# Delta-net layer of a decoder step: the norm of a head's output in two groups of chunks, on VectorE but for the power

## The chip, the cores and the metric

The kernel runs on one core of a Trainium2 chip. The metric is the device time of one execution in microseconds; the median of three runs before the change is 3306.21 us (3305.95 to 3306.49).

## The reference

One inference step of a two-layer decoder, for a prompt of 1024 tokens and, beside it, 8 sequences of 8 new tokens each (64 rows). Layer 0 mixes tokens with a gated delta net, layer 1 with windowed attention, and both end in a feed-forward block. Only the delta net's output norm is touched by the change. For each of 8 heads (128 wide) the recurrence is

```
def step(s, xs):
    w_c, u_c, attn_c, q_c, k_c, ge_c = xs
    u = u_c - jnp.einsum('bhcd,bhde->bhce', w_c, s)
    o = jnp.einsum('bhcd,bhde->bhce', q_c, s) + jnp.einsum('bhcs,bhse->bhce', attn_c, u)
    s = ge_c[..., None, None] * s + jnp.einsum('bhcd,bhce->bhde', k_c, u)
    return s, o
...
o = rms_norm(o, o_gain) * jax.nn.silu(gate...)
y = o.reshape(b, l, A_V_DIM).astype(h.dtype) @ w_out
```

`rms_norm` divides each token's row of `o` by the root of its mean square plus 1e-6. In the kernel `q` is not normalised before the recurrence, so its inverse length `rq` (one number per token, with the factor 1/sqrt(128)) enters in the norm: the mean square is multiplied by `rq` twice, and the factor applied to the row is the power -0.5 of that, times `rq` again.

## The kernel before, in words

Tokens lie in nine chunks: eight of 128 rows for the prompt, one of 64 for the new tokens (`NT`, `tok`). The delta net (`gdn`) is a pipeline over heads. In step `i` of its loop three generators run merged: `gdn_scan` of head `i-2` (the recurrence, its decode part, the norm and the output), `gdn_prep` of head `i-1` (squares, the inverse of the chunk matrix, `kdec`, `vs`, `aT`), and `gdn_dense` of head `i` (three projections of 72 matmuls each in three pieces of columns, 384, 352 and 352, with the convolution `yc` on VectorE). The `yield` values decide which generator goes next; after that the compiler's scheduler places every instruction in the queue of its engine by its own estimates, and each engine works through its queue in that order. So an instruction that waits holds back all that stands behind it in its queue. Six steps (heads 0 to 5 of the order) have all three generators; in the last two the dense work has ended and the gate projections stand in its place.

What the prediction speaks of, by name:

- `o` shares its tile with `vs`, so the profile writes `vs` for both. L1210 adds up chunk `c` of the output (`vs<-t,C`), L1201 updates the state `S`, L1188 makes `r`, L1186 is the product of the keys with `S`.
- L1223 squares a chunk on ScalarE and sums it into a column of `ss_o`. L1224 to L1228, all on GpSimd (POOL), turn nine columns into the factor `f_o`; L1227 is the power. L1231 multiplies `o` by `f_o`, also on POOL. L1239 transposes the chunks on TensorE (PE) into `ot` (bank tag `C`), and `ot` goes to DRAM.
- L1068 transposes `E` into `F` on VectorE (DVE), and L1074 `B<-F,NZ` is the first product with it, in the inversion of the next head's chunk matrix. Its results pass through ScalarE and VectorE and come back to PE as `B<-Y,Dx`.
- L1141 multiplies `kqm` on POOL for the decode part of the next scan, from `qT` and `kT`, which SP loads by DMA. L144 makes the low part `w` of the next weights, L978 evicts `kdec` from PSUM, which frees a bank for L1007 `A<-kT`.
- L983 subtracts in `aT`, whose rows come by a broadcast DMA from `gcd`.

The instructions of the norm, in the order of the code:

```
nc.gpsimd.tensor_tensor(ss, ss, rq, op=ALU.mult)
nc.gpsimd.tensor_tensor(ss, ss, rq, op=ALU.mult)
nc.gpsimd.tensor_scalar(ss, ss, 1.0 / P, EPS, op0=ALU.mult, op1=ALU.add)
nc.gpsimd.tensor_tensor(f, ss, half, op=ALU.pow)
nc.gpsimd.tensor_tensor(f, f, rq, op=ALU.mult)
```

Of the kernel before, what the change touches and what calls it, by code (L numbers as in the profile page):

```python
# [16 lines left out]
AF = mybir.ActivationFunctionType  # L17
ALU = mybir.AluOpType
# [4 lines left out]
P = 128  # L23
# [4 lines left out]
SD = DB * DL  # L28
T = SP + SD
NT = 9  # L30
FF = 2816
NF = FF // P
EPS = 1e-6
# [6 lines left out]
def tok(tt):  # L40
    return (tt * P, P) if tt < 8 else (SP, SD)
# [592 lines left out]
class Gdn:  # L634
# [473 lines left out]
    def gdn_scan(self, v, wk, slot, m, st, og, qkv, delta_p, delta_s, on, oT):  # L1108

        nc = self.nc  # L1110
        ident, hd = self.ident, v["hd"]
        kdec, vs, aT, T2, bcol, rq = (v[x] for x in ("kdec", "vs", "aT", "T2", "bcol", "rq"))
        ge, gam, ngam = st["ge"], st["gam"], st["ngam"]
        bc = lambda col, s, rows=P, n=P: col[:rows, s][:, :, None].to_broadcast([rows, s.stop - s.start, n])
        parts = ((slice(0, 8), P), (slice(8, 9), SD))

        def rtile(name, bufs=2):
            return wk.tile([P, P], F32, tag=name, name=name, bufs=bufs)

        def small(name):  # L1120
            return wk.tile([P, NT], F32, tag=name, name=name, bufs=2)

        def quad(name):
            return wk.tile([P, 4, P], F32, tag="quad", name=name, bufs=4)
# [4 lines left out]
        o = vs  # L1129
        S = None  # L1130

        def decode():
            sd, kq = [], []
            for g in range(2):
                s_d, kqm = quad("s_d"), quad("kqm").rearrange("p b (x t) -> p b x t", x=2)
                sd.append(s_d)
                kq.append(kqm)
                nc.sync.dma_start(s_d, v["state"][:, 4 * g:4 * g + 4])
                q8 = m["Q8"][:, 4 * g:4 * g + 4].rearrange("p b c l -> p b (c l)")
                for x, f in ((0, kT), (1, qT)):  # L1140
                    nc.gpsimd.tensor_tensor(kqm[:, :, x], f[:, None, SP:T].to_broadcast([P, 4, SD]), q8, op=ALU.mult)  # L1141
            yield
            p1 = self.bank("C")
            for g in range(2):
                for b in range(4):
                    nc.tensor.matmul(p1[:, :P], kq[g][:, b].rearrange("p x t -> p (x t)"), sd[g][:, b],
                                     start=g + b == 0, stop=g == 1 and b == 3)
            r = rtile("rd", 1)
            nc.vector.scalar_tensor_tensor(r[:SD], p1[:SD, :P], ngam[:SD, 8, hd:hd + 1], vs[:SD, 8], op0=ALU.mult, op1=ALU.add)
            t = rtile("td", 1)  # L1150
            nc.scalar.activation(t[SD:], p1[SD:, :P], AF.Copy, scale=gam[SD:, 8, hd:hd + 1])
            yield
            p2 = self.bank("C")
            nc.tensor.matmul(p2[:SD, :P], T2[:SD, 8, :SD], r[:SD], start=True, stop=True)
            u = rtile("ud", 1)
            nc.scalar.activation(u[:SD], p2[:SD, :P], AF.Copy, scale=bcol[:SD, 8:9])
            yield
            p4 = self.bank("C")
            nc.tensor.matmul(p4[:SD, :P], aT[:SD, 8, :SD], u[:SD], start=True, stop=True)
            nc.vector.tensor_add(o[:SD, 8], p4[:SD, :P], t[SD:])  # L1160
            yield
            ums = []
            for g in range(2):
                b4 = slice(4 * g, 4 * g + 4)
                um = quad("um")[:SD]
                ums.append(um)
                nc.vector.tensor_tensor(um, u[:SD][:, None, :].to_broadcast([SD, 4, P]),
                                        m["sel8"][:, b4, None].to_broadcast([SD, 4, P]), op=ALU.mult)
                nc.gpsimd.tensor_tensor(sd[g], sd[g], ge[:, 1, b4, hd][:, :, None].to_broadcast([P, 4, P]), op=ALU.mult)
            yield  # L1170
            for g in range(2):
                b4 = slice(4 * g, 4 * g + 4)
                p3 = self.bank("C")
                w = p3.rearrange("p (b d) -> p b d", d=P)
                nc.tensor.matmul(w, kdec[:SD, 8], ums[g], start=True, stop=True)
                nc.vector.tensor_add(sd[g], sd[g], w)
                nc.sync.dma_start(delta_s[b4, hd].rearrange("b k v -> k b v"), sd[g])
                yield

        dec = decode()  # L1180
        for c in range(8):
            t0 = c * P
            r = vs[:, c]
            if c:
                p1 = self.bank("C")
                nc.tensor.matmul(p1[:, :P], kT[:, t0:t0 + P], S, start=True, stop=True)  # L1186
                r = rtile("r")
                nc.vector.scalar_tensor_tensor(r, p1[:, :P], ngam[:, c, hd:hd + 1], vs[:, c], op0=ALU.mult, op1=ALU.add)  # L1188
                yield 0.02
                next(dec, None)  # L1190
                yield 0.01
            p2 = self.bank("C")
            nc.tensor.matmul(p2[:, :P], T2[:, c], r, start=True, stop=True)
            u = rtile("u")
            nc.scalar.activation(u, p2[:, :P], AF.Copy, scale=bcol[:, c:c + 1])
            yield 0.03
            p3 = self.bank("C")
            nc.tensor.matmul(p3[:, :P], kdec[:, c], u, start=True, stop=True)
            So, S = S, rtile("S")
            if c:  # L1200
                nc.vector.scalar_tensor_tensor(S, So, ge[:, 0, c, hd:hd + 1], p3[:, :P], op0=ALU.mult, op1=ALU.add)  # L1201
            else:
                nc.vector.tensor_copy(S, p3[:, :P])
            p4 = self.bank("C")
            nc.tensor.matmul(p4[:, :P], aT[:, c], u, start=True, stop=True)
            if c:
                nc.tensor.matmul(p4[:, P:2 * P], qT[:, t0:t0 + P], So, start=True, stop=True)
                t = rtile("t1")
                nc.scalar.activation(t, p4[:, P:2 * P], AF.Copy, scale=gam[:, c, hd:hd + 1])
                nc.vector.tensor_add(o[:, c], t, p4[:, :P])  # L1210
            else:
                nc.vector.tensor_copy(o[:, c], p4[:, :P])
            yield 0.03
        nc.sync.dma_start(delta_p[hd], S)
        for _ in dec:
            pass
        half = self.mhalf[:, :NT]
        ss, f = small("ss_o"), small("f_o")
        nc.gpsimd.memset(ss, 1.0)
        for c in range(NT):  # L1220
            n = tok(c)[1]
            j = rtile("junk")
            nc.scalar.activation(j[:n], o[:n, c], AF.Square, accum_out=ss[:n, c:c + 1])  # L1223
        nc.gpsimd.tensor_tensor(ss, ss, rq, op=ALU.mult)  # L1224
        nc.gpsimd.tensor_tensor(ss, ss, rq, op=ALU.mult)
        nc.gpsimd.tensor_scalar(ss, ss, 1.0 / P, EPS, op0=ALU.mult, op1=ALU.add)
        nc.gpsimd.tensor_tensor(f, ss, half, op=ALU.pow)  # L1227
        nc.gpsimd.tensor_tensor(f, f, rq, op=ALU.mult)  # L1228
        yield 0.1
        for s, n in parts:  # L1230
            nc.gpsimd.tensor_tensor(o[:n, s], o[:n, s], bc(f, s, n), op=ALU.mult)  # L1231
        yield 0.1
        ot = slot("ot", "kT2").rearrange("p a b -> p (a b)")
        for c0, c1 in GR:
            ps = self.bank("C")
            n = 0
# [645 lines left out]
```

## Time and profile before

| what | value |
|---|---|
| median of three runs | 3306.21 us |
| the profiled execution | 3316.33 us |
| its span in the profile | 3314.6 us |
| mean granted clock of TensorE | 0.967 of full speed |
| busy share PE / DVE / ACT / POOL | 94% / 65% / 46% / 41% |

The span runs from the first to the last instruction that the profiler saw; 1.7 us of the execution lie around it. The delta net takes roughly the stretch from 60 to 790 us. Busy shares are means over stages with different limits. A timeline row gives the start in us from the span's start, the duration, the engine, the line, the operation with its output and inputs, the shape, how often it stands there, and in brackets the idle time of the engine before it with what ended it. The granted clock is a share of 2.4 GHz: 1.00 is 2.4 GHz and 0.50 is 1.2 GHz.

### The profile page before, as it was taken

The page shows a single profiled execution, that of the slowest core. Times are in us where ns is not written, and L with a number is a line of the kernel's source. Part 1 is how long each engine was busy: PE and PEld are TensorE (multiplying, and loading weights), DVE is VectorE, ACT ScalarE, POOL GpSimd, SP SyncE. Part 2 cuts the span into 40 slices and gives each one's busy share as a digit, 9 for nine tenths or more (in the row PEclk, how much of TensorE's full clock was granted, in tenths as well). Part 3 has the DMA queues.
Part 4 walks back from the last instruction along what each step waited for, and adds up shares of the span by engine and source line. Part 5 has one row for each costly group of instructions (what it writes and reads, how often), then busy time and mean ns, then how long its engine had stood idle before and what let it go on. Part 6 is the DMA issues. An engine that isn't in the chain of part 4 may idle for free. (4 is left out here: it accounts for less than half of the span.)

```text
span 3314.6 us, 54654 instructions
## 1 busy us (share of the span) xinstructions
PE 3101.6 (94%) x20072; PEld 2841.4 (86%) x20072; DVE 2154.9 (65%) x4483; ACT 1527.0 (46%) x3739; POOL 1354.0 (41%) x1374
## 2 busy tenths in 40 slices
PE   7899999999999999999999999998898999999997
PEld 7888888888789999987788988888586999998785
DVE  5676676633666666566847777677746666665766
ACT  5444455433533333244547676767334333332344
POOL 3233333333456666544531223130114566664543
PEclk9999999999999999999999999999889999999998
DMA  4333333345322222363451111111443122224534
GB/s 136 95 109 101 101 101 101 103 130 172 124 73 90 98 98 91 130 200 86 140 164 47 33 54 53 35 54 52 156 130 118 65 98 98 97 96 151 168 104 131
DMA packets 283752, 346.42 MB, mean 105 GB/s; under 512 B 43330, under 2 KB 218802, under 8 KB 280668
## 3 DMA queue, kind: packets, MB, share of 16 engines
q1 hardware_dynamic: 271612, 293.51, 28.7%
q0 software_dynamic: 11728, 48.87, 3.8%
q8 instruction: 158, 2.59, 0.3%
q14 instruction: 110, 0.90, 0.1%
q10 hardware_dynamic: 144, 0.56, 0.0%
HBM read 245.21 MB, written 97.66 MB: 103 GB/s over the span
## 5 line engine op out<-in xcount | busy, mean ns | idle before, releaser
L784 PE MATMUL mm<-h_hi,w 128*128 128x352 f32 (+1 forms) x1536 | 444.9, 349 | 11.0 <-ACT xr L821 8.6
L451 PE MATMUL acc<-wa,ga 128*128 128x512 f32 x1716 | 418.5, 398 | 23.4 <-ACT wa L389 14.2
L451 PEld LDWEIGHTS acc<-wa,ga 128*128 128x128 f32 x1716 | 326.4, 192 | 102.8 <-ACT wa L389 15.8
L1366 PE MATMUL mm<-h_hi,w 128*128 128x352 f32 (+1 forms) x1152 | 353.8, 342 | 0.0
L784 PEld LDWEIGHTS mm<-h_hi,w 128*128 128x128 f32 x1536 | 283.6, 193 | 23.0 <-ACT xr L821 9.5
L784 PE MATMUL mm<-h_lo,w 128*128 128x352 f32 (+1 forms) x768 | 260.1, 339 | 0.0
L303 DVE TENSOR_TENSOR s<-w,s 128x512 fp32r<-128x512 f32 x132 | 190.9, 1447 | 101.8 <-ACT s L302 101.6
L302 ACT ACTIVATE s<-t 128x512 fp32r<-128x512 f32 x176 | 110.8, 630 | 301.5 <-PE mm L354 287.9
L390 DVE TENSOR_TENSOR ga<-graw,ga 128x512 fp32r<-128x512 f32 (+2 forms) x176 | 153.0, 874 | 131.0 <-ACT ga L389 130.7
L322 POOL TENSOR_TENSOR wide<-wide,v 128x288 f32<-128x288 f32 (+1 forms) x176 | 148.2, 842 | 199.5 <-DVE v L321 199.1
L389 ACT ACTIVATE ga<-graw 128x512 fp32r<-128x512 f32 (+2 forms) x176 | 100.9, 576 | 259.1 <-PE acc L451 234.4
L1457 ACT ACTIVATE s<-s,stat 128x128 f32<-128x128 f32 (+1 forms) x384 | 169.6, 443 | 95.4 <-DVE stat L1455 93.5
L1366 PEld LDWEIGHTS mm<-h_hi,w 128*128 128x128 f32 x1152 | 211.8, 189 | 1.6
L144 POOL TENSOR_TENSOR w<-raw,w 128x1024 fp32r<-128x1024 f32 x38 | 100.5, 2646 | 244.7 <-ACT w L141 162.6
L303 DVE TENSOR_TENSOR s<-t,s 128x512 fp32r<-128x512 f32 x176 | 161.7, 920 | 46.1 <-ACT s L302 45.8
L1366 PE MATMUL mm<-h_lo,w 128*128 128x352 f32 (+1 forms) x576 | 189.1, 328 | 0.0
L587 PE MATMUL mm<-mw_hi,o_hl 128*128 128x512 f32 x544 | 177.3, 403 | 3.9 <-ACT o_hl L575 3.9
L293 POOL TENSOR_TENSOR t<-w 128x512 f32<-128x512 f32 x88 | 115.2, 1311 | 146.5 <-DVE s L303 65.1
L1474 DVE TENSOR_TENSOR pl<-tr,ph 128x256 fp32r<-128x256 f32 (+1 forms) x192 | 104.6, 545 | 105.1 <-ACT ph L1473 104.0
L354 PE MATMUL mm<-b0h,s 128*128 128x256 f32 (+1 forms) x704 | 145.2, 293 | 12.2 <-ACT s L302 9.5
L831 DVE SCALAR_TENSOR_TENSOR yc<-xr,convw,yc 128x1112 f32<-128x1112 f32 x72 | 115.5, 1604 | 54.5 <-ACT yc L829 54.4
L784 PEld LDWEIGHTS mm<-h_lo,w 128*128 128x128 f32 x768 | 149.1, 194 | 1.9 <-issue 0.9
(474 smaller groups left out, 9329.4 us busy)
## 6 DMA issues: line engine op xcount, KB each, us to landing
w<-in_ffn_w_in_dram SPq DMA_DIRECT2D x88, 512.0 KB
graw<-gs SPq DMA_DIRECT2D x143, 256.0 KB
gs<-wide POOLq DMA_DIRECT2D x22, 1024.0 KB, 4.2
gs<-wide POOLq DMA_DIRECT2D x66, 256.0 KB, 2.6
raw<-in_a_w_in_dram SPq DMA_DIRECT2D x32, 512.0 KB
qkv<-f SPq DMA_DIRECT2D x24, 544.0 KB
xo<-x SPq DMA_DIRECT2D x24, 512.0 KB
raw<-in_b_w_q_dram SPq DMA_DIRECT2D x24, 512.0 KB
```

The lines of the kernel that those rows point to most:

```text
L293: op(t, x, y)
L302: nc.scalar.activation(out[j][:, 0], x, AF.Copy)
L303: nc.vector.tensor_sub(out[j][:, 1], x, out[j][:, 0])
L322: nc.gpsimd.tensor_tensor(out, out, v, op=ALU.mult)
L354: nc.tensor.matmul(ps[:, :HC[c][1]], u, v, start=z == 0, stop=z == 11)
L390: nc.vector.tensor_sub(t[:, 1, :n], x, t[:, 0, :n])
L451: nc.tensor.matmul(acc[i], g[:, u, c], w[:, v], start=p == 0 and n == 0, stop=p == NP - 1 and n == 2)
L587: nc.tensor.matmul(ps, a, b[:, k], start=k == 0 and i == 0, stop=k == KD - 1 and i == len(seq) - 1)
L784: nc.tensor.matmul(ps[:, :n], a[:, k, :], b[:, k, n0:n0 + n], start=i_ == 0, stop=i_ == 23)
L831: nc.vector.scalar_tensor_tensor(yc, xr[:, j:j + CW], w(j), yc, op0=ALU.mult, op1=ALU.add)
L1366: nc.tensor.matmul(ps[:, :n], a[:, k, :], b[:, k, n0:n0 + n], start=i == 0, stop=i == 23)
L1457: nc.scalar.activation(s[:, a, :n], s[:, a, :n], AF.Exp, bias=m, scale=-1.0, accum_out=stat[:, 1, a, b:b + 1])
```

## The change

The nine columns of the norm are made in two groups: chunks 0 to 3 while the scan is at chunk 5 (their scaling at chunk 6), and chunks 4 to 8 at the end. The three small multiplications and the multiply-add go to VectorE, and so does the scaling of `o`; the power stays on GpSimd. The memset of `ss_o` moves to the start of the scan.

```diff
--- before.py
+++ after.py
@@ -1112,7 +1112,6 @@
         kdec, vs, aT, T2, bcol, rq = (v[x] for x in ("kdec", "vs", "aT", "T2", "bcol", "rq"))
         ge, gam, ngam = st["ge"], st["gam"], st["ngam"]
         bc = lambda col, s, rows=P, n=P: col[:rows, s][:, :, None].to_broadcast([rows, s.stop - s.start, n])
-        parts = ((slice(0, 8), P), (slice(8, 9), SD))
 
         def rtile(name, bufs=2):
             return wk.tile([P, P], F32, tag=name, name=name, bufs=bufs)
@@ -1177,8 +1176,35 @@
                 nc.sync.dma_start(delta_s[b4, hd].rearrange("b k v -> k b v"), sd[g])
                 yield
 
+        half = self.mhalf[:, :NT]
+        ss, f = small("ss_o"), small("f_o")
+        nc.gpsimd.memset(ss, 1.0)
+
+        def norm(c0, c1):
+
+            s = slice(c0, c1)
+            for c in range(c0, c1):
+                n = tok(c)[1]
+                j = rtile("junk")
+                nc.scalar.activation(j[:n], o[:n, c], AF.Square, accum_out=ss[:n, c:c + 1])
+            for _ in range(2):
+                nc.vector.tensor_tensor(ss[:, s], ss[:, s], rq[:, s], op=ALU.mult)
+            nc.vector.tensor_scalar(ss[:, s], ss[:, s], 1.0 / P, EPS, op0=ALU.mult, op1=ALU.add)
+            nc.gpsimd.tensor_tensor(f[:, s], ss[:, s], half[:, s], op=ALU.pow)
+            nc.vector.tensor_tensor(f[:, s], f[:, s], rq[:, s], op=ALU.mult)
+            yield
+            for x, n in ((slice(c0, min(c1, 8)), P), (slice(max(c0, 8), c1), SD)):
+                if x.start < x.stop:
+                    nc.vector.tensor_tensor(o[:n, x], o[:n, x], bc(f, x, n), op=ALU.mult)
+
         dec = decode()
         for c in range(8):
+            if c == 5:
+                mid = norm(0, 4)
+                next(mid)
+            if c == 6:
+                for _ in mid:
+                    pass
             t0 = c * P
             r = vs[:, c]
             if c:
@@ -1214,21 +1240,11 @@
         nc.sync.dma_start(delta_p[hd], S)
         for _ in dec:
             pass
-        half = self.mhalf[:, :NT]
-        ss, f = small("ss_o"), small("f_o")
-        nc.gpsimd.memset(ss, 1.0)
-        for c in range(NT):
-            n = tok(c)[1]
-            j = rtile("junk")
-            nc.scalar.activation(j[:n], o[:n, c], AF.Square, accum_out=ss[:n, c:c + 1])
-        nc.gpsimd.tensor_tensor(ss, ss, rq, op=ALU.mult)
-        nc.gpsimd.tensor_tensor(ss, ss, rq, op=ALU.mult)
-        nc.gpsimd.tensor_scalar(ss, ss, 1.0 / P, EPS, op0=ALU.mult, op1=ALU.add)
-        nc.gpsimd.tensor_tensor(f, ss, half, op=ALU.pow)
-        nc.gpsimd.tensor_tensor(f, f, rq, op=ALU.mult)
+        end = norm(4, NT)
+        next(end)
         yield 0.1
-        for s, n in parts:
-            nc.gpsimd.tensor_tensor(o[:n, s], o[:n, s], bc(f, s, n), op=ALU.mult)
+        for _ in end:
+            pass
         yield 0.1
         ot = slot("ot", "kT2").rearrange("p a b -> p (a b)")
         for c0, c1 in GR:
```

The scheduler's order moves with it. First POOL at the end of a head. Before (L1224 to L1231 are the norm; `kqm` follows them):

```order
L144 TENSOR_TENSOR w<-raw,w 128x1024
L996 MEMSET nc 64x16
L1224 TENSOR_TENSOR ss_o<-ss_o,rq 128x9
L1225 TENSOR_TENSOR ss_o<-ss_o,rq 128x9
L1226 TENSOR_SCALAR ss_o<-ss_o 128x9
L1227 TENSOR_TENSOR f_o<-ss_o,mhalf 128x9
L1228 TENSOR_TENSOR f_o<-f_o,rq 128x9
L1219 MEMSET ss_o 128x9
L1231 TENSOR_TENSOR vs<-vs,f_o 128x1024
L1231 TENSOR_TENSOR vs<-vs,f_o 64x128
L1141 TENSOR_TENSOR kqm<-qT_2303,Q_501 128x4x64
```

With the change:

```order
L144 TENSOR_TENSOR w<-raw,w 128x1024
L996 MEMSET nc 64x16
L1140 TENSOR_TENSOR kqm<-qT_2309,Q_501 128x4x64
L815 MEMSET xr 128x3
L1193 TENSOR_TENSOR f_o<-ss_o,mhalf 128x5
L1181 MEMSET ss_o 128x9
```

All of the norm but the power has left this queue, and `kqm` and a memset of `xr` now stand ahead of the power of the last five columns.

VectorE at the end of a head, from `Dx` to the group of `aT`. Before:

```order
L1052 TENSOR_TENSOR Dx<-dc,sel_458 128x1024
L831 SCALAR_TENSOR_TENSOR yc<-xr,convw,yc 128x1112
L1052 TENSOR_TENSOR Dx<-dc,sel_458 64x64
L816 COPY xr<-hist 128x8x3
L1079 TENSOR_TENSOR E<-dc,par 128x256
L983 SCALAR_TENSOR_TENSOR aT<-aT,gc,U 128x128
L1068 STREAM_TRANSPOSE F<-E 128x256
L983 SCALAR_TENSOR_TENSOR aT<-aT,gc,U 128x128 x7
```

With the change:

```order
L1052 TENSOR_TENSOR Dx<-dc,sel_458 128x1024
L1052 TENSOR_TENSOR Dx<-dc,sel_458 64x64
L1191 TENSOR_TENSOR ss_o<-ss_o,rq 128x5
L1079 TENSOR_TENSOR E<-dc,par 128x256
L1192 TENSOR_SCALAR ss_o<-ss_o 128x5
L983 SCALAR_TENSOR_TENSOR aT<-aT,gc,U 128x128
L1194 TENSOR_TENSOR f_o<-f_o,rq 128x5
L1068 STREAM_TRANSPOSE F<-E 128x256
L1198 TENSOR_TENSOR vs<-vs,f_o 128x512
L1198 TENSOR_TENSOR vs<-vs,f_o 64x128
L983 SCALAR_TENSOR_TENSOR aT<-aT,gc,U 128x128 x7
```

The three steps ahead of the power are put between older instructions; the multiplication of `f_o`, which needs the power, stands ahead of the transposition into `F`.

VectorE in the scan, where the first group is made. Before:

```order
L1034 TENSOR_TENSOR vs<-A,ivk 128x512
L1040 STREAM_SHUFFLE row<-dc 128x144
L1201 SCALAR_TENSOR_TENSOR S<-S,ge,C 128x128
L1041 TENSOR_TENSOR row<-row,nc 128x9x4
L1042 TENSOR_TENSOR dc<-dc,row 128x9x4
L1040 STREAM_SHUFFLE row<-dc 128x144
```

With the change:

```order
L1034 TENSOR_TENSOR vs<-A,ivk 128x512
L1192 TENSOR_SCALAR ss_o<-ss_o 128x4
L1040 STREAM_SHUFFLE row<-dc 128x144
L1194 TENSOR_TENSOR f_o<-f_o,rq 128x4
L1227 SCALAR_TENSOR_TENSOR S<-S,ge,C 128x128
L1041 TENSOR_TENSOR row<-row,nc 128x9x4
L1198 TENSOR_TENSOR vs<-vs,f_o 128x512
L1042 TENSOR_TENSOR dc<-dc,row 128x9x4
```

The multiplication of `f_o` stands ahead of the state `S`, and the scaling of four chunks behind it. On PE the chunk transposes at the end of a head were one group of six ahead of `B<-F,NZ`:

```order
L784 MATMUL mm<-h_hi,w 128x352
L1239 MATMUL C<-ident,vs 128x128 x6
L1074 MATMUL B<-F,NZ 128x128 x8
L1074 MATMUL B<-Y,Dx 128x128 x4
L784 MATMUL mm<-h_hi,w 128x352
```

With the change:

```order
L784 MATMUL mm<-h_hi,w 128x352
L1255 MATMUL C<-ident,vs 128x128 x2
L784 MATMUL mm<-h_hi,w 128x352
L784 MATMUL mm<-h_lo,w 128x352
L784 MATMUL mm<-h_hi,w 128x352
L1255 MATMUL C<-ident,vs 128x128 x2
L784 MATMUL mm<-h_hi,w 128x352
L784 MATMUL mm<-h_lo,w 128x352
L784 MATMUL mm<-h_hi,w 128x352
L1074 MATMUL B<-F,NZ 128x128 x8
L1074 MATMUL B<-Y,Dx 128x128 x4
L1255 MATMUL C<-ident,vs 128x128 x4
```

Four transposes and six dense matmuls now stand ahead of `B<-F,NZ`, and the other transposes behind it.

## Rows read from the trace of the kernel before

**Rows 1.** Waits of PE from 100 to 780 us: us in all, times, longest.
```profile
PE C L1239 <- POOL vs L1231: 26.0, 7, 4.1
PE A L1007 <- DVE kdec L978: 11.6, 6, 2.0
```

**Rows 2.** Timeline of PE, second of six like heads: start, us, instruction, [idle before].
```profile
289.33 0.48 PE L784 MATMUL mm<-h_hi,w 128*128 128x352 f32 x2
289.65 0.32 PE L784 MATMUL mm<-h_lo,w 128*128 128x352 f32 x1
...
294.25 1.54 PE L1239 MATMUL C<-ident,vs 128*128 128x128 f32 x6 [4.11 <-POOL vs L1231]
295.58 0.64 PE L1074 MATMUL B<-F,NZ 128*128 128x128 f32 x2
```

**Rows 3.** Timeline of POOL in the same stretch.
```profile
289.27 2.65 POOL L1227 TENSOR_TENSOR f_o<-ss_o,mhalf 128x9 f32<-128x9 f32 x1
...
292.30 2.30 POOL L1231 TENSOR_TENSOR vs<-vs,f_o 128x1024 f32<-128x1024 f32 x2
294.57 0.72 POOL L1141 TENSOR_TENSOR kqm<-qT,Q 128x256 f32<-128x256 f32 x1
```

**Rows 4.** Timeline of DVE in the same stretch.
```profile
289.05 1.21 DVE L1052 TENSOR_TENSOR Dx<-dc,sel 128x1024 f32<-128x1024 f32 x1
...
291.74 0.42 DVE L1079 TENSOR_TENSOR E<-dc,par 128x256 f32<-128x256 f32 x1
292.32 2.03 DVE L983 SCALAR_TENSOR_TENSOR aT<-aT,gc,U 128x128 f32<-128x128 f32 x1 [0.16 <-DMA aT<-gcd]
294.27 0.43 DVE L1068 STREAM_TRANSPOSE F<-E 128x256 f32<-128x256 f32 x1
```

**Rows 5.** Timelines of DVE, POOL and PE, fourth like head, after the end.
```profile
476.83 3.31 DVE L831 SCALAR_TENSOR_TENSOR yc<-xr,convw,yc 128x1112 f32<-128x1112 f32 x1
475.47 3.49 POOL L144 TENSOR_TENSOR w<-raw,w 128x1024 fp32r<-128x1024 f32 x1 [2.78 <-ACT w L141]
481.40 0.49 PE L1007 MATMUL A<-kT 128*128 128x128 f32 x2 [2.01 <-DVE kdec L978]
```

**Rows 6.** Stretches: busy us, granted clock (PEclk), DMA share, GB/s.
```profile
242.40:245.70 3.30, 3.29 (x14) 3.30 (x15) 1.87 (x8) 0.75 (x2) 2.84 (x6) 0.50 1.05 346
481.40:484.70 3.30, 3.29 (x27) 3.30 (x28) 2.54 (x9) 1.09 (x3) 2.84 (x6) 1.00 1.05 346
```

**Rows 7.** Timeline of DVE in the scan of the second head.
```profile
268.54 0.20 DVE L1029 TENSOR_SCALAR rq<-rq 128x9 f32<-128x9 f32 x1 [0.38 <-POOL rq L1028]
...
270.30 0.69 DVE L1034 TENSOR_TENSOR vs<-A,ivk 128x512 f32<-128x512 f32 x1 [0.20 <-PE A L954]
...
271.17 0.35 DVE L1201 SCALAR_TENSOR_TENSOR S<-S,ge,C 128x128 f32<-128x128 f32 x1
```

**Rows 8.** Timeline of PE there.
```profile
271.74 0.38 PE L1186 MATMUL C<-S,kT 128*128 128x128 f32 x2
```

**Rows 9.** Power of 1 column and of 9 on POOL, by line: duration min/median/max.
```profile
L153 POOL TENSOR_TENSOR rstd<-rstd,mhalf x72: 541/549/1602, 7.1 to 3307.3; 128x1 f32<-128x1 f32 x64, 64x1 f32<-64x1 f32 x8
L1028 POOL TENSOR_TENSOR rq<-nq,mhalf x8: 1794/1796/2975, 115.8 to 666.3; 128x9 f32<-128x9 f32 x8
```

**Rows 10.** DMA packets, second head, 290.3 to 293.5 and 293.5 to 293.6 us.
```profile
DMA packets 956, 0.96 MB, mean 299 GB/s; under 512 B 48, under 2 KB 828, under 8 KB 956
DMA packets 59, 0.03 MB, mean 302 GB/s; under 512 B 0, under 2 KB 59, under 8 KB 59
```

**Rows 11.** DMA packets, fifth like head, 528.8 to 532.7 us.
```profile
DMA packets 950, 0.98 MB, mean 251 GB/s; under 512 B 48, under 2 KB 815, under 8 KB 950
```

**Rows 12.** Timeline of POOL, fifth like head.
```profile
533.62 0.78 POOL L1141 TENSOR_TENSOR kqm<-qT,Q 128x256 f32<-128x256 f32 x1 [0.93 <-DMA qT<-qkv]
534.34 0.10 POOL L815 MEMSET xr<- 128x3 f32 x1
```

**Rows 13.** Timeline of PE, last head.
```profile
761.74 0.66 PE L1239 MATMUL C<-ident,vs 128*128 128x128 f32 x4 [1.33 <-POOL vs L1231]
```

## The prediction

> **What bounds the kernel now.** The profile's first part (the table above) has PE busy for 94% of the span, so the question is what PE waits for where the change is made. The view of PE's waits over the delta net names two. It waited 26.0 us in seven places for POOL's scaling of `o` (tile `vs`, L1231) and 11.6 us in six for `kdec` [rows 1]. The timelines show the first: at the end of the second head PE issues its last dense product at about 290.1 and then stands still for 4.11 us, because the transposes of L1239 are next in its queue [rows 2]. POOL meanwhile works through the power of nine columns, 2.65 us, and the scaling, 2.30 us [rows 3]. Six heads are alike in this. Two more facts from the same stretch count. VectorE's `aT` at 292.32 takes 2.03 us beside POOL's scaling, so `F` comes only at 294.27, and PE's `B<-F,NZ` could start at 295.58 without waiting [rows 2, 4]. And `kqm` follows the scaling on POOL at once [rows 3].
>
> The second wait comes later in the step. VectorE's `yc` takes 3.31 us beside POOL's `w` of 3.49 us, `kdec` stands behind it, and PE waits 2.01 us [rows 5]. Of two such places the stretch behind one ran at a granted clock of 0.50 (1.2 GHz) for 3.3 us, the one shown from the fourth head at 1.00 (2.4 GHz) [rows 6].
>
> **Part one, the first group, during the scan.** Removed: nothing here. Added: four short operations on VectorE, the power of four columns on POOL and the scaling of 512 elements a row on VectorE. The order has `f_o<-f_o,rq` ahead of the state `S`, and it needs the power. So the chain is: the last `vs<-A` ends at 270.30 + 0.69 = 270.99; the multiply-add takes 0.20, as `rq` did [rows 7]; the power takes, by 549 ns for one column and 1796 ns for nine, 0.549 + 3 x 0.156 = 1.02 us [rows 9]; the multiplication 0.20; then `S`, 0.35 [rows 7]. `S` would end at 270.99 + 0.20 + 1.02 + 0.20 + 0.35 = 272.76. The product with the keys, which started at 271.74 without idle time [rows 8], would start at about 272.8: 1.05 us later, and everything on PE behind it too, since PE's order has the same two dense products ahead of it as before. Queued behind the waiting multiplication are `S`, the `row` and `dc` steps of the next head and the scaling. The scaling itself costs 0.69, as `vs<-A` of the same shape [rows 7]; it stands behind `S` and I cost it at nothing, since six dense products and a decode product lie between `C<-S,kT` and the next product that needs VectorE. Without that cover it is 0.7 more. The least is 0 (if the scheduler's dense work hides all), the most about 1.75. I take 1.05, the chain's own sum: **six heads, +6.3 us**.
>
> **Part two, the end of a head.** Removed from POOL: three small multiplications, a multiply-add, four columns of the power and the scaling. VectorE gets the small ones and the scaling of five chunks, behind `F`, and PE takes the transposes of finished chunks first, then six dense products, then `B<-F,NZ`. If this were all, the stall would be gone. But POOL's queue now has `kqm` and a memset ahead of the power, and `kqm` needs `qT` from DMA, while VectorE's `f_o` stands ahead of `F`, which PE's next product needs. So a load decides. In the second head it moved as packets between 2 and 8 KB: 956 less 828 is 128 of them from 290.3 to 293.5, and none in the tenth behind (59 of 59 are smaller) [rows 10]. In the fifth head the packets of this size end by 532.7 as well (950 less 815: the 128 and 7 of the next transfer) [rows 11], and there `kqm` did wait for `qT`, and started at 533.62 [rows 12], 0.9 us behind the last packet. With the same 0.9, `qT` is there at 294.4 in the second head: just before `kqm` started, at 294.57, and not earlier.
>
> The chain is then: `kqm` at 294.45, 0.72 long [rows 3]; the memset, 0.10 [rows 12]; the power of five columns, 0.549 + 4 x 0.156 = 1.17 [rows 9]; the multiplication, 0.20 [rows 7]; `F`, 0.43 [rows 4]. That gives 297.07, so `B<-F,NZ` starts at about 297.1 and not at 295.58: +1.5. PE has six dense products less to do behind it, at 0.48 - 0.32 = 0.16 each [rows 2], so 0.94 are won; two transposes more are left for later, at 1.54 / 6 = 0.26 by row or some 0.22 with the overlap of their ends, so 0.44 are lost [rows 2]. Net 1.5 - 0.94 + 0.44 = 1.0. The least is 0.05: `kqm` at 293.5, at once on the last packet. The most is 2.0: in the fifth head the load came 0.9 behind the scaling's end instead of level with it [rows 12]. I take 1.0, since the second head's load is the one whose packets and start both stand in the rows: **six heads, +6.0 us**. The stall of PE does not go, it changes its name: some 5.5 us for `F` from VectorE.
>
> On VectorE the end costs 0.69 for 512 elements and about 0.28 for the new tokens; both stand behind `F` and beside PE's own products of the inversion, so nothing. At 65% busy VectorE has the room.
>
> **Part three, `kdec`.** `kqm` from `kT` and `w` change places on POOL, and the dense products that were pulled forward are missing as filler there. The wait of 2.0 us [rows 1] may go from nothing lost to all gone: -12 to +6 us over six heads. The nearest row is the wait as it is, so I keep it, but in heads where the clock fell behind it a shift decides, and a stretch of 3.3 us at half clock [rows 6] is 1.65 us dearer. I take **-2.0 us** in all, about one such stretch.
>
> **Part four, the last head.** There is no next head to prepare, and PE waits 1.33 us for the scaling [rows 13]. On VectorE with half the chunks done that goes: **-1.3 us**.
>
> **The sum.** 6.3 + 6.0 - 2.0 - 1.3 = +9.0 us. The sum is made against the profiled execution, 3316.33 us (span 3314.6 and 1.7 around), which gives 3325.3. That execution stands 10.1 above the median of the runs, 3306.21, so on the median it is **3315.2 us**.
>
> **A rule against the rows.** Both a rule and this sum speak of the same scaling. By the rows it took 2.30 us on POOL [rows 3], and VectorE multiplied as many elements a row (1024) in 1.21 [rows 4]. The Trainium skill, "GPSIMD Engine Reference", § 4.1 Engine selection, puts elementwise work with two inputs on VectorE and calls it about twice slower on GpSimd; these two rows agree. By the exchange alone the sum would be, per head, 2.30 - 1.21 = 1.1 and 2.65 - 1.17 = 1.5 for the shorter power, 2.6 less, and 15.6 + 1.3 = 16.9 less in all: 3289.3. I go by the queue instead, because an instruction's price matters only if it starts on time.
>
> **The rivals.** *The end is shorter after all* (0.2). If `qT` lands before POOL wants it, the power starts on its inputs: `E` ends at 291.74 + 0.42 = 292.16 [rows 4], the multiply-add at 292.36, power 293.53, multiplication 293.73, `F` 294.16, `B<-F` about 294.2: -1.4 - 0.94 + 0.44 = -1.9 a head. Then 6.3 - 11.4 - 2.0 - 1.3 = -8.4, or 3297.8. It decides from the point where `qT` is there by about 291.5, 2.9 us earlier than now. For it: nothing forbids the other loads to shift. Against it: the packets [rows 10, 11]. The exchange by itself (3289.3) is its far end.
>
> *The mid group costs little and the `kdec` wait halves* (0.25). If PE's dense work takes up all but 0.3 us of the late `S`, and a shorter queue on POOL takes `w` from beside `yc` in half the heads, it is 1.8 + 6.0 - 6.0 - 1.3 = +0.5, or 3306.7: no change. For it: `yc` beside `w` is a matter of 2 us [rows 5]. Against it: PE had no idle time ahead of `C<-S,kT` [rows 8], so its order is tight there.
>
> *The clock falls more often* (0.1). The stall at the end grows and one is added in the scan. If each new one is followed by a stretch at half clock, as behind `kdec` [rows 6], six times 1.65 come on top: 3325.1. Against it: the stretch from the fourth head stayed at 1.00 behind a longer wait than the new one in the scan.
>
> **How the numbers follow.** The forecast has 0.45. A measurement of this kernel tells about 0.2% from no change, 6.6 us. Faster by more: the first rival, 0.2. Within: the second, 0.25, and the forecast's lower part where the end costs its least, 0.05, so 0.3. Slower by more: the rest of the forecast and the third, 0.5. The forecast's own range is 3306 to 3321; with the rivals and the end at its most, 3294 to 3326.
>
> **What would show it.** Right: in the changed kernel PE waits for VectorE's `F` at `B<-F,NZ` in six places, over 5 us each, in place of POOL's `vs`; POOL's `kqm` has idle time for `qT` ahead of it and the power starts behind; PE waits about 1 us at one `C<-S,kT` in each of six heads. Wrong: no wait at `B<-F,NZ`, or a power that runs before `kqm` could; no wait in the scan; a wait for `kdec` that is gone, or a new one elsewhere in the queue of VectorE.

## The result, and the profile after

The changed kernel took 3324.69 us in the median of five runs (3319.43 to 3333.98), against 3306.26 for the kernel before: a ratio of 1.0053 (95% interval 1.0035 to 1.0071). Measured once more later, beside the experiments, it took 3320.31 us against 3307.31, a ratio of 1.0032 (1.0019 to 1.0045). So it is slower by 0.2 to 0.7%, some 13 to 18 us; the forecast was 9 us slower. The first median lies above the forecast's own range of 3306 to 3321 us and inside the wide one of 3294 to 3326; the second lies in both. The runs of the kernel before itself spread from 3297 to 3321 us in the later sessions, so only ratios over many runs are compared below.

The profiled execution of the changed kernel has a span of 3318.1 us, only 3.5 more than that of before, which was itself 10 us above its median. The stretch from `B<-F,NZ` of the first like head to that of the last head tells more. It holds nearly the same work in both, and here stands with its length, the busy times of PE, PE's weight loads, VectorE, ScalarE and POOL (with counts of instructions), the granted clock, DMA share and GB/s, first before the change:

```profile
216.40:693.70 477.30, 437.10 (x2932) 401.81 (x2932) 326.57 (x912) 237.46 (x736) 165.68 (x204) 0.96 0.33 103
```

and after it:

```profile
213.30:701.10 487.80, 440.64 (x2926) 403.25 (x2927) 325.29 (x978) 236.60 (x735) 139.47 (x177) 0.95 0.32 101
```

It is 10.5 us longer (7.0 in the second profile of the changed kernel). PE stands idle 7.0 us more (47.2 for 40.2; 4.1 in the second profile) and is busy 3.5 us longer with nearly the same instructions, at a lower clock (2.9 in the second). POOL is busy 26 us less, and that bought nothing. What PE waited for in the delta net, in us, with times and longest, after the change:

```profile
PE B L1074 <- DVE F L1068: 21.7, 6, 3.9
PE mm L784 <- ACT xr L821: 13.4, 8, 2.9
PE C L1212 <- DVE S L1229: 6.0, 3, 2.0
PE C L1212 <- DVE S L1227: 5.2, 8, 0.8
...
PE A L1007 <- DVE kdec L978: 3.6, 3, 1.8
```

The 26.0 us for POOL's scaling [rows 1] are gone by name. In their place stand 21.7 for `F`, six new waits for `xr` (the list had two waits of 4.8 us for `xr` before), and 5.2 for the state `S`. The 11.6 for `kdec` [rows 1] have become 3.6, but 6.0 for the first `S` of a head are new. (In the second profile it is 20.5 for `F`, 5.4 for `S`, 6.2 for `kdec` and 2.4 for the first `S`.)

The second head shows how. PE's timeline, which answers to [rows 2]:

```profile
288.83 0.38 PE L1255 MATMUL C<-ident,vs 128*128 128x128 f32 x2
290.74 0.43 PE L784 MATMUL mm<-h_hi,w 128*128 128x352 f32 x1 [1.53 <-ACT xr L821]
...
295.92 3.75 PE L1074 MATMUL B<-F,NZ 128*128 128x128 f32 x16 [3.73 <-DVE F L1068]
```

VectorE in the same stretch [rows 4]:

```profile
291.03 0.16 DVE L1192 TENSOR_SCALAR ss_o<-ss_o 128x5 f32<-128x5 f32 x1
291.60 0.35 DVE L983 SCALAR_TENSOR_TENSOR aT<-aT,gc,U 128x128 f32<-128x128 f32 x1 [0.41 <-DMA aT<-gcd]
295.26 0.17 DVE L1194 TENSOR_TENSOR f_o<-f_o,rq 128x5 f32<-128x5 f32 x1 [3.31 <-POOL f_o L1193]
295.34 0.44 DVE L1068 STREAM_TRANSPOSE F<-E 128x256 f32<-128x256 f32 x1
295.70 0.84 DVE L1198 TENSOR_TENSOR vs<-vs,f_o 128x512 f32<-128x512 f32 x2
```

and POOL [rows 3]:

```profile
293.33 0.72 POOL L1140 TENSOR_TENSOR kqm<-qT,Q 128x256 f32<-128x256 f32 x1 [5.32 <-DMA qT<-qkv]
293.99 0.11 POOL L815 MEMSET xr<- 128x3 f32 x1
294.05 1.17 POOL L1193 TENSOR_TENSOR f_o<-ss_o,mhalf 128x5 f32<-128x5 f32 x1
```

Read from below: POOL stands idle for 5.32 us, because `kqm` waits for `qT`. The input of the power is ready at 291.19 and the power starts at 294.05. VectorE waits 3.31 us for it with `F` behind, although `E` was done at 291.1. (This head lies some 1.2 us earlier than in the profile before: POOL's `w` ahead of it ends at 284.31 here and at 285.47 there. So `kqm`'s 293.33 answers to the 294.45 of the forecast.) PE waits 3.73 us for `F`. Ahead of that PE waits 1.53 us for `xr`, a wait that the prediction did not have. ScalarE's timeline says why:

```profile
289.11 1.06 ACT L833 ACTIVATE f<-yc 128x1024 f32<-128x1024 f32 x1 [5.40 <-DVE yc L831]
290.07 0.24 ACT L835 ACTIVATE f<-yc 128x64 f32<-128x64 f32 x1
290.22 0.82 ACT L821 ACTIVATE xr<-mm 128x384 f32<-128x384 f32 x2
```

The eviction of `xr` would free a PSUM bank for the six dense products that were pulled forward, but the activation `f<-yc` stands ahead of it and waits for the end of VectorE's `yc`.

In the scan, VectorE and POOL, answering to [rows 7]:

```profile
268.71 0.16 DVE L1192 TENSOR_SCALAR ss_o<-ss_o 128x4 f32<-128x4 f32 x1
270.06 0.16 DVE L1194 TENSOR_TENSOR f_o<-f_o,rq 128x4 f32<-128x4 f32 x1 [0.95 <-POOL f_o L1193]
270.14 0.34 DVE L1227 SCALAR_TENSOR_TENSOR S<-S,ge,C 128x128 f32<-128x128 f32 x1
```

```profile
269.02 1.01 POOL L1193 TENSOR_TENSOR f_o<-ss_o,mhalf 128x4 f32<-128x4 f32 x1 [2.56 <-DVE ss_o L1192]
```

and PE, answering to [rows 8]:

```profile
270.54 0.49 PE L1212 MATMUL C<-S,kT 128*128 128x128 f32 x2 [0.83 <-DVE S L1227]
```

### The profile page after: what moved, and what is told of

Read it like the earlier page. It is cut to its first block, busy times and chain, and to the rows that moved or that the text cites. A ratio compares the mean times of both kernels' runs of the same rounds, so it can differ in the third digit from the quotient of the medians.

```text
span 3318.1 us, 54702 instructions
## 1 busy us (share of the span) xinstructions
PE 3096.2 (93%) x20072; PEld 2833.2 (85%) x20072; DVE 2156.9 (65%) x4571; ACT 1525.7 (46%) x3739; POOL 1317.9 (40%) x1334
## 5 line engine op out<-in xcount | busy, mean ns | idle before, releaser
L354 PE MATMUL mm<-b6h,s 128*128 128x256 f32 (+1 forms) x704 | 142.9, 292 | 5.1 <-ACT b6h L189 5.1
```

The source lines that it names most:

```text
L354: nc.tensor.matmul(ps[:, :HC[c][1]], u, v, start=z == 0, stop=z == 11)
```

## The experiments

Two theories stood against each other. **The queue**: the norm's factor waits for a load on POOL, and the state and `F` stand behind that factor on VectorE; the exchange of engines is not at fault. **The rival**: the extra work on VectorE and the products pulled forward are the loss, or the wait only moves on. The orders were mended with `issue_after`, which puts an instruction behind another in its engine's queue and changes no data.

**`kqm` behind the power.**

```diff
-                    nc.gpsimd.tensor_tensor(kqm[:, :, x], f[:, None, SP:T].to_broadcast([P, 4, SD]), q8, op=ALU.mult)
+                    with self.tc.issue_after(self.pw.ins) if hasattr(self, "pw") else nullcontext():
+                        nc.gpsimd.tensor_tensor(kqm[:, :, x], f[:, None, SP:T].to_broadcast([P, 4, SD]), q8, op=ALU.mult)
...
-            nc.gpsimd.tensor_tensor(f[:, s], ss[:, s], half[:, s], op=ALU.pow)
+            self.pw = nc.gpsimd.tensor_tensor(f[:, s], ss[:, s], half[:, s], op=ALU.pow)
```

> Changed kernel, but POOL's kqm of the next head is ordered behind the power of the norm, so that the power no longer stands behind a wait for the load of qT; everything else is free. Theory (the load on the path: kqm waits for qT ahead of the power, F stands behind it): the power starts when the multiply-add is done, PE's waits for F fall from 3.6 to about 0.9 us in each of six heads, 16 us less, about 3308 us. It should also make the runs agree with each other more closely than the 3319 to 3334 of the changed kernel, since the landing of a load no longer sets the time. Rival (the waits for xr of 1.5 us, the one for S of 0.8 us and the extra work on VectorE are the loss): no less than 3320 us.

Measured: 3298.14 us, ratio 0.9969 (0.9957 to 0.9981): faster than the kernel before. PE's waits there:

```profile
PE mm L784 <- ACT xr L821: 13.7, 8, 3.5
PE B L1074 <- DVE F L1068: 6.2, 6, 1.1
```

The wait for `F` is 1.0 us a head, as worked out. POOL's queue shows the load in its new place, where it holds nobody up:

```profile
287.61 1.17 POOL L1194 TENSOR_TENSOR f_o<-ss_o,mhalf 128x5 f32<-128x5 f32 x1 [2.02 <-DVE ss_o L1193]
289.06 0.72 POOL L1141 TENSOR_TENSOR kqm<-qT,Q 128x256 f32<-128x256 f32 x1 [0.29 <-DMA qT<-qkv]
```

The waits for `F` account for 15.5 us. By the ratios more than that was won, some 21 to 28 us, and the stretch between the same two marks runs at a higher clock, 0.98 for 0.95:

```profile
213.10:679.60 466.50, 431.77 (x2926) 392.39 (x2927) 328.23 (x978) 236.30 (x735) 141.25 (x179) 0.98 0.34 106
```

That is one profile of each. Over all runs the clock of a whole execution is 0.973 on the mean for these twelve, and 0.969 for the twelve of the unaltered changed kernel below, so the gain of clock is not of the profiled execution alone. The waits for `xr` and `S` stayed as they were, so the rival's explanation falls. One part of my expectation falls too: the runs spread from 3289 to 3309 us, no less than those of the kernel before, so the spread of the changed kernel's runs is not from this load.

**The state ahead of the factor, in the scan.** The multiplication of `f_o` for chunks 0 to 3 is issued behind `S` of that step.

```diff
-            nc.vector.tensor_tensor(f[:, s], f[:, s], rq[:, s], op=ALU.mult)
-            yield
+            if c0 == 0:
+                yield
+            with self.tc.issue_after(last_s.ins) if c0 == 0 else nullcontext():
+                nc.vector.tensor_tensor(f[:, s], f[:, s], rq[:, s], op=ALU.mult)
+            if c0:
+                yield
...
-                nc.vector.scalar_tensor_tensor(S, So, ge[:, 0, c, hd:hd + 1], p3[:, :P], op0=ALU.mult, op1=ALU.add)
+                last_s = nc.vector.scalar_tensor_tensor(S, So, ge[:, 0, c, hd:hd + 1], p3[:, :P], op0=ALU.mult, op1=ALU.add)
```

> Changed kernel, but in the scan the multiplication of f_o for the first group stands behind the state S on VectorE, so S does not wait for the power of four columns. Theory (the hold of S is a term by itself, 0.83 us in six heads): about 5 us less, 3319.7 us, and the waits of PE at the product of the keys with S behind the mid group are gone. Rival (PE meets the next wait instead, and nothing is won): 3324 us, with a new wait of about 0.8 us in each head.

Measured: 3314.86 us, ratio 1.0020 (1.0008 to 1.0032). The waits for this `S` fell from 5.2 us in eight places to 1.8 in two; 1.8 us of a new kind came in five:

```profile
PE B L1074 <- DVE F L1068: 20.8, 6, 4.3
...
PE C L1174 <- DVE vs L1240: 1.8, 5, 0.4
PE C L1216 <- DVE S L1231: 1.8, 2, 1.4
```

The direction is the theory's, but against the second measurement of the unaltered kernel (1.0019 to 1.0045) the intervals overlap, so the time does not tell the size of this term. By these two rows 1.6 us are won and not 5: some of what the rival expected, a next wait, did come.

**One group only, all on VectorE but the power.** No work is left out; the first group is made with the rest.

```diff
-            if c == 5:
-                mid = norm(0, 4)
-                next(mid)
-            if c == 6:
-                for _ in mid:
-                    pass
...
-        end = norm(4, NT)
+        end = norm(0, NT)
```

> No first group: all nine columns at the end, small operations and scaling on VectorE, the power on GpSimd; the compiler's order is free (F then stands ahead of the multiplication of f_o on VectorE, kqm still ahead of the power on POOL, and PE's transposes of the chunks come behind B<-F). Theory (kqm does harm only because F stands behind the power): no wait at B<-F, no hold of S, no wait for xr; against the kernel before the 26 us of waits at the transposes go, less a few us of waits for kdec and of low clock, about 3286 us. Rival (the work added to VectorE delays the inversion and the evictions there): 3306 us or more.

Measured: 3313.62 us, ratio 1.0018 (1.0004 to 1.0031). The theory was wrong by 27 us, and the time is where the rival had it, at 3306 or more. The waits:

```profile
PE B L1074 <- DVE F L1068: 18.8, 6, 3.6
PE A L1007 <- DVE kdec L978: 11.5, 6, 2.0
PE B L1074 <- DVE F L1083: 7.6, 6, 1.5
```

`F` stands ahead of the factor here, and PE waits about 3 us for it all the same. VectorE's timeline of the second head shows a chain with hardly a gap: `yc`, the small piece of `Dx`, `E`, `F`, with the small operations of the norm between them.

```profile
283.95 1.37 DVE L831 SCALAR_TENSOR_TENSOR yc<-xr,convw,yc 128x1112 f32<-128x1112 f32 x1
285.24 0.21 DVE L1052 TENSOR_TENSOR Dx<-dc,sel 64x64 f32<-64x64 f32 x1
...
285.59 0.42 DVE L1079 TENSOR_TENSOR E<-dc,par 128x256 f32<-128x256 f32 x1
...
286.34 0.44 DVE L1068 STREAM_TRANSPOSE F<-E 128x256 f32<-128x256 f32 x1
290.19 0.17 DVE L1194 TENSOR_TENSOR f_o<-f_o,rq 128x9 f32<-128x9 f32 x1 [3.42 <-POOL f_o L1193]
```

The three small operations of the norm take up some 0.2 us of that chain, by the starts of what follows them; the rest of it stood there before as well. So the old stall of 4.11 us [rows 2] covered most of a second one of about 3 us: with the transposes out of the way PE arrives at `B<-F,NZ` before VectorE has `F`. And the factor still holds VectorE's queue for 3.42 us, now with the second round's `F` (L1083) behind it.

**The unaltered change once more.**

> The changed kernel once more, unaltered, so that it stands beside the others with the same runs of the kernel before. All theories: 0.35 to 0.7% above the kernel before, as the first time, with six waits of PE for F of about 3.6 us and six for xr of 1.5 us.

Measured: 3320.31 us, 1.0032 (1.0019 to 1.0045); the waits for `F` are 20.5 us in six places.

**One group, with `kqm` behind the power**: both edits above together.

> One group of nine columns at the end on VectorE as in the run before last, but POOL's kqm ordered behind the power. Theory (PE's 3.0 us before B<-F there are a floor that VectorE's own work ahead of F sets, with or without the norm; what kqm costs is the 1.2 us before the second round of B<-F, since f_o holds VectorE's queue): the waits for F at L1068 stay at about 18 us in six heads, those for F at L1083 fall from 7.6 to under 2; about 6 us less than the 3313.6 us there. Rival (kqm's wait for qT is also what holds the first F): both waits fall, 20 us less.

Measured: 3306.94 us, 0.9999 (0.9988 to 1.0010), 7 us less than without the order.

```profile
PE B L1074 <- DVE F L1068: 19.6, 6, 4.1
PE A L1007 <- DVE kdec L978: 11.6, 6, 2.0
...
PE B L1074 <- DVE F L1083: 1.5, 1, 1.5
```

The 3 us before the first `F` stay, those before the second go: they are set by VectorE's own chain, and the load acts only through the queue. Moving the work between engines, without a first group and without harm from the queue, is worth nothing measurable.

**`F` ahead of the factor, in two groups.** The multiplication of `f_o` at the end is issued behind the transposition into `F`; `kqm` stays ahead of the power.

```diff
-            nc.vector.transpose(out=out.rearrange("p c j -> p (c j)"), in_=x.rearrange("p c j -> p (c j)"))
+            self.fturn = nc.vector.transpose(out=out.rearrange("p c j -> p (c j)"), in_=x.rearrange("p c j -> p (c j)"))
...
-            nc.vector.tensor_tensor(f[:, s], f[:, s], rq[:, s], op=ALU.mult)
-            yield
+            if c0:
+                yield
+            with self.tc.issue_after(self.fturn.ins) if c0 and hasattr(self, "fturn") else nullcontext():
+                nc.vector.tensor_tensor(f[:, s], f[:, s], rq[:, s], op=ALU.mult)
+            if c0 == 0:
+                yield
```

> Changed kernel, but at the end of a head the multiplication of f_o stands behind F on VectorE; kqm keeps its place ahead of the power on POOL. Theory (the loss is that F waits, not that the norm is late): the 21.7 us of waits for F go, about 3303 us, though POOL still waits for qT. Rival (the wait goes over to the transposes, which need the same factor): PE waits for the scaled vs, 2 to 3 us in each head, 3315 us or more.

Measured: 3295.00 us, 0.9960 (0.9947 to 0.9973). The waits for `F` went from 21.7 to 1.6 us, though POOL still waits for `qT`:

```profile
PE mm L784 <- ACT xr L821: 13.2, 8, 2.9
PE C L1216 <- DMA kT<-qkv: 10.4, 5, 2.6
...
PE B L1074 <- DVE F L1068: 1.6, 3, 1.2
```

The transposes did not take the wait over, but another came: 10.4 us for the load of `kT` in five heads. In the code `ot` lies in the slot of that `kT`, so the load has to wait until `ot` is stored, and in the order `ot`'s transposes now come behind the inversion's first products. In the first head SP issues that store at 225.39 us and the load at 229.71; in the changed kernel it was 223.45 and 227.29, about 4 us apart in both. That this is the whole cause was not tried. The stretch between the two marks runs at a clock of 0.99:

```profile
211.90:669.00 457.10, 424.36 (x2928) 386.86 (x2929) 322.01 (x979) 235.47 (x736) 130.26 (x181) 0.99 0.34 109
```

**All three orders mended, and then ScalarE's too.** The first of these has the power ahead of `kqm`, `F` ahead of the factor and `S` ahead of the first factor. The second adds:

```diff
-                    nc.scalar.activation(xr[:, 3 + n0:3 + a1], ps[:, :a1 - n0], AF.Copy)
+                    with self.tc.high_priority():
+                        nc.scalar.activation(xr[:, 3 + n0:3 + a1], ps[:, :a1 - n0], AF.Copy)
```

and the same for the other eviction of `xr`, so that they stand ahead of `f<-yc`.

> The changed kernel with all three orders mended: kqm behind the power, f_o of the end behind F, f_o of the first group behind S. Theory (the holds are separate terms): against f_o behind F alone, 3295.0 us, the waits of 0.83 us for S go: 5 us less, 3290 us. Rival (PE only comes earlier to its next wait, the load of kT at the product with S, which was 10.4 us there): 3295 us with that wait grown by about 5 us.

> The run before with, besides, the evictions of xr ahead of the f activations in ScalarE's queue, so that PE's dense products at the end of a head find their PSUM bank free. Theory (each of the six waits of 1.53 us is only that queue): 9 us less than that run, about 3281 us if that one is 3290. Rival (PE then waits as much longer for F, since VectorE's chain up to F is the floor there): the same time, with waits for F of about 1.5 us in six heads.

Measured: 3289.18 us, 0.9938 (0.9926 to 0.9950), and 3284.30 us, 0.9927 (0.9913 to 0.9941). The first is where the theory had it; the waits for `S` are down to 1.4 us and that for `kT` is 10.2, no longer than before. But this run has `kqm` behind the power as well, its interval touches that of `F` alone (0.9947 to 0.9973), and 1.8 us of waits for `vs` came as in the run with `S` alone; so what is won over `F` alone is not shown to be the wait for `S`. Of the second, the waits:

```profile
PE C L1215 <- DMA kT<-qkv: 9.4, 5, 2.3
PE mm L784 <- ACT xr L822: 7.7, 7, 3.1
PE B L1075 <- DVE F L1069: 6.5, 6, 2.1
```

Those for `xr` fell by 5.8 us (from 13.5) and those for `F` rose by 5.6 (from 0.9): here the rival is right, VectorE's chain sets when `F` is there. The times of the two can't be told apart. Both beat the kernel before, by 0.6 to 0.7%, and the changed one by about 1%.

## Why the prediction was right

The sign, the place and the mechanism were right: +13 to +18 us measured, +9.0 forecast. The size is within the wide range, but the first of the two measurements lies above the forecast's own range. Step by step:

- **The first group: +6.3 forecast, about +4.5 measured.** The power took 1.01 us for 1.02, the product with the keys waited 0.83 us for 1.05 in five heads and 0.31 in the sixth; the other two waits of the 5.2 us lie elsewhere. The scaling of 512 elements behind `S` cost PE nothing in the six like heads, as assumed; in the next head it takes 1.42 us ahead of `r`, and PE's wait there is 2.60 us for 1.87 before.
- **The end: +6.0 forecast, +6.2 by the waits** (21.7 and six times 1.53, less six times 4.11). In the second head PE stood 5.26 us where the sum had some 5.1. But what it stood for was named only in part: the sign given for it, a wait for `F` of over 5 us in each of six places, did not come; those waits are 3.4 to 3.9. The step "six dense products less to do behind it" took it that they run at once; they waited 1.53 us for `xr`. POOL's stall had covered that wait, which the sum should have named. It changed no sum only because `F` came later still.
- **`qT` decides: right.** The hold of POOL's queue, read from packets that were still moving [rows 10, 11], is the 5.32 us of idle time ahead of `kqm`. Putting `kqm` behind the power turned 1.0032 into 0.9969. It decides only because `F` stands behind the factor, as the prediction said: with `F` ahead, POOL still waits and the loss is gone.
- **`kdec`: a wait that moved.** The 11.6 us became 3.6 for `kdec`, 0.6 for it at L954 and 6.0 for the first `S`: 1.4 less (2.5 in the second profile). The prediction had named a new wait elsewhere in VectorE's queue as a sign of being wrong, and this is one. It is the same collision in another place. In the fourth head, VectorE and POOL [rows 5]:

```profile
480.24 3.58 DVE L831 SCALAR_TENSOR_TENSOR yc<-xr,convw,yc 128x1112 f32<-128x1112 f32 x1
483.75 0.28 DVE L1229 COPY S<-C 128x128 f32<-128x128 f32 x1
```

```profile
480.27 2.37 POOL L144 TENSOR_TENSOR w<-raw,w 128x1024 fp32r<-128x1024 f32 x1
```

  `yc` takes 3.58 us beside `w` where the next one takes 1.36; the copy of `S` stands behind it and PE waits 1.99 us. The Trainium skill, "SBUF — State Buffer", § Who interferes with whom, states that a VectorE instruction with two inputs in SBUF and a GpSimd instruction that reads SBUF exclude each other; the difference of 2.2 us is nearly the 2.37 of `w`, so the trace agrees.
- **The clock: a term that the sum lacked.** The -2.0 stood for one stretch of half clock less behind `kdec`, and there it came: four such stretches of some 3.4 us before, three behind the wait for `S` now (one in the second profile). But the sum has no term for the clock at the end of a head. There the stretches at 0.50 (1.2 GHz) grew from 27 us in six heads to 38, in both profiles. In the third head, before and after, a stretch some 4 and 2 us behind the end of PE's wait (which ended at 374.8 and 376.7):

```profile
378.90:382.20 3.30, 3.30 (x30) 3.11 (x28) 0.51 (x2) 1.58 (x5) 0.00 (x0) 1.00 0.53 174
```

```profile
379.10:382.40 3.30, 3.30 (x18) 3.30 (x17) 0.98 (x6) 2.04 (x3) 0.00 (x0) 0.50 0.29 66
```

  Between the two marks PE is busy 3.5 us longer (2.9 in the second profile) with nearly the same instructions: an estimate of what the clock cost, where 2.0 were put down as won. This is in part the third rival, which put 9.9 us on it.
- **The last head: -1.3, as forecast.** Its transposes have no wait in front of them any more.

The waits that the sum named make 4.5 + 6.2 - 1.4 - 1.3 = +8.0 us where it had 11.0 (some 6 in the second profile), and the clock some +3 where it had -2.0. So the sum of about 11 us lies near the forecast's 9.0 in part by luck, since one error went against the other. It is near the lower of the two measured differences; what is left to the 18 us of the first was not settled, and the two profiled executions, whose totals differ by 3.5 us only, can't settle it.

The first rival (the end gets shorter) fell with the load. What was wrong in it is shown by the one-group runs: even with the factor out of the way, PE waits 3 us for VectorE's own chain. The second (the wait for `kdec` halves) fell with the wait for the first `S` that took its place. The rule by which elementwise work belongs on VectorE ("GPSIMD Engine Reference" of the Trainium skill, § 4.1 Engine selection) has the direction of the price: the scaling of nine chunks took 1.41 us on VectorE (in the one-group run) and 2.30 on POOL [rows 3], a factor of 1.6 rather than two. The time was set by the queues.

## What to carry to other kernels

When a step is split over two engines, look at what the scheduler puts ahead of its slow half and behind its fast half: here a multiplication that waits for a load stood ahead of the power, and the state and `F` stood behind the factor, and three edges of order turned a change that lost 0.3 to 0.5% into one that gains 0.6%; either of the two at the end of a head, alone, made it gain 0.3 to 0.4%. A stall of the critical engine may cover others that would come next (3 us for `F`, 1.5 for an eviction), so the gain of removing it is what is left above those, not its length.

## What was not expected of the hardware

The clock was worth nearly as much as some of the waits, and it did not go by their length alone. Between the marks it was 0.95 in the changed kernel, with waits of 3.4 to 3.9 us at `B<-F` and one of 1.5 us for `xr` ahead of each; 0.98 with waits of about 1 us there; and 0.99 with `F` ahead of the factor, the longest wait 2.6 us. But in the one-group run, with single waits of 2.5 to 3.6 us at `B<-F`, it was 0.98 as well: there the six ends of a head had 3.4 us each at 0.50, where in the changed kernel five of the six had 6.8. What makes the one or the other was not tried. Shortening six waits by 2.6 us each won 5 to 12 us more, by the ratios, than the 15.5 that the waits themselves held.
